# First chunk's pool mixer and layer norm ahead of the others, its first three FFN products between their stages

## The chip, the cores and the metric

The kernel runs on one core of a Trainium2 chip. The metric is the device time of one execution in microseconds (us). Engines are named as in the profile: PE (TensorE matmul), PEld (its weight loads), DVE (VectorE), ACT (ScalarE), POOL (GpSimd), and SP (SyncE), whose queue issues the DMA transfers.

## The reference

One inference step of a two-layer decoder trunk for 1024 prompt tokens, 16 meta tokens and 8 sample tokens, model width 1024, in float32. Layer 0 mixes by causal pooling (trailing means over 2, 4, 8 and 16 tokens in four groups of channels, each followed by a 256x256 projection); layer 1 by sliding-window attention. Every layer then has a gated FFN with a short convolution.

```python
mix = pool_mixer(x, w_pool, scale)          # window mean minus token, projected per group
x = layer_norm(ALPHA * x + mix, g, b)
gu = x @ w_in                               # 1024 -> 2 * 2816
g, u = gu[..., :D_FF], gu[..., D_FF:]
c = conv_b + sum(shift(g, k) * conv_w[k] for k in range(3))
h = silu(c) * u
x = layer_norm(ALPHA * x + h @ w_out, g2, b2)
...
```

## The kernel before, in words

Features lie on the 128 partitions, tokens on the free axis. The tokens are cut into three chunks: chunk 0 has 280 columns (16 meta, 8 samples, 256 prompt tokens), chunks 1 and 2 have 384 each. Every product of the FFN is three matmuls, because weights and activations are split into a high and a low part (`mm3`, lines 115 to 122). The high part of a weight is an ACT cast (line 111) and its low part a POOL subtraction (line 112), both from a raw tile that SP has loaded (line 105). Raw tiles have two buffers in all (tag `raw`), and the pool mixer's inputs (`praw`, line 247) use the same two.

The first phase makes, for each chunk in the order of the source:

- the pool mixer `pool_chunk` (line 273): running sums `pt` on DVE and POOL (line 292; group 3 and every third stage of a group are POOL's), the differences `pd` on DVE (lines 303 to 314), projections `pp` on PE (line 325), and `zp` on DVE (line 326). A chunk has eight `zp` tiles;
- the layer norm `ln_steps` (line 187): the mean `ps_mum` on PE (line 143), the subtraction (line 188, DVE), squares (line 192, ACT), the variance `ps_varm` on PE, the reciprocal root by Ln and Exp (lines 200 and 201, ACT), the scaling (line 224 on DVE, or line 211 on POOL for the tiles in `on_pool`), then the high part `xh` (line 232, ACT) and the low part `xl` (line 233 on DVE, line 222 on POOL).

Then `ffn(0)` (line 354) begins with the first three of 22 column blocks f of the FFN, chunk by chunk: `ffn1(f, c)` (line 361) makes the gate product `pg` and the up product `pu` with 24 matmuls each, copies the gate to SBUF (ACT), convolves it (POOL line 378, DVE lines 379 to 381 for chunk 0), and makes h (silu on ACT line 398, DVE lines 399 and 402, ACT line 401). From block 3 on the loops run block by block over all chunks, with the output products `po` between.

A scheduler orders the instructions of each engine at build time, from the order of the source and its own timing model; on the chip every engine runs its list in that order and waits where an input is missing. `tc.issue_after(ins)` keeps a block's instructions on the engine of `ins` behind it. In what follows a name such as `pt_1_0` carries the chunk and the tile, `pg_0_1` the block and the chunk; the last number of a name in an ordered list is that of a buffer.

Of the kernel before, what the change touches and what calls it, by code (L numbers as in the profile page):

```python
# [10 lines left out]
ALU = mybir.AluOpType  # L11
# [16 lines left out]
# prompt blocks (of 128 tokens) per chunk; the first chunk also carries the  # L28
# meta tokens and the sample tokens: columns [meta 16 | samples 8 | prompt]
# [6 lines left out]
# columns alive after the attention: [meta14 meta15 | samples 8 | prompt]  # L36
# [3 lines left out]
# packed per-partition constant columns  # L40
# [7 lines left out]
# constants of the first phase alone  # L48
# [11 lines left out]
def trunk_kernel(ctx: ExitStack, tc: tile.TileContext, ins: dict, outs: dict):  # L60
# [19 lines left out]
    # ------------------------------------------------------------ constants  # L80
# [34 lines left out]
    def mm3(out, wts, movs):  # L115
        """out += sum_k w_k^T x_k over exact hi/lo parts (all but lo*lo)."""
        n = len(wts)
        for k in range(n):
            (wh, wl), (mh, ml) = wts[k], movs[k]
            nc.tensor.matmul(out, lhsT=wh, rhs=mh, start=(k == 0), stop=False)  # L120
            nc.tensor.matmul(out, lhsT=wh, rhs=ml, start=False, stop=False)  # L121
            nc.tensor.matmul(out, lhsT=wl, rhs=mh, start=False, stop=(k == n - 1))  # L122
# [7 lines left out]
    # ----------------------------------------------------------- layer norm  # L130
    def colsum(parts, W, name, on_pe, own=False, split=False, pairs=False, step=KT):
        """mean over all features of 8 [P, W] tiles -> PSUM, on every partition; pauses after every step tiles."""
        ps = bank(f"ps_{name}", "ln")[:, :W]
        if on_pe:
            # fp32 products; with pairs, of sums of two tiles
            n = KT // 2 if pairs else KT
            for k in range(n):
                if pairs:
                    t = hslot([P, W], f"pr{k}_{name}", F32)
                    (nc.gpsimd if k < n // 2 else nc.vector).tensor_tensor(t, parts(2 * k), parts(2 * k + 1), ALU.add)  # L140
                else:
                    t = parts(k)
                nc.tensor.matmul(ps, lhsT=r32(ones), rhs=t, start=(k == 0), stop=(k == n - 1))
            return ps
        s = [None, None]
        for m in range(0, KT, 2):
            # two chains of sums, so that one is ready while the other's last ends
            i = m // 2 % 2
            a, b = parts(m), parts(m + 1)
            eng = nc.vector if split and i else nc.gpsimd  # L150
            if s[i] is None:
                s[i] = a if own else ltmp([P, W], f"s{i}_{name}")
                eng.tensor_tensor(s[i], a, b, ALU.add)
            else:
                eng.tensor_tensor(s[i], s[i], a, ALU.add)
                eng.tensor_tensor(s[i], s[i], b, ALU.add)
            if (m + 2) % step == 0 and m + 2 < KT:
                yield
# [19 lines left out]
    def ln_steps(z, W, lni, c, xo, name, out=None, on_pe=False, on_pool=(), lnexp=False, split=False, fin=False):  # L178
        # a list of tiles in the place of x, which gets new ones
# [18 lines left out]
        if lnexp:  # L198
            # both functions share a table set with the softmax's
            nc.scalar.activation(rstd, var, AF.Ln, bias=epsc)  # L200
            nc.scalar.activation(rstd, rstd, AF.Exp, scale=-0.5)
        else:
            nc.scalar.activation(rstd, var, AF.Sqrt, bias=epsc)
            nc.vector.reciprocal(rstd, rstd)
        yield
        for m in range(KT):
# [16 lines left out]
            else:  # L223
# [6 lines left out]
                else:  # L230
                    h, l = xh[c][m][:, xo:xo + W], xl[c][:, m, xo:xo + W]
                    nc.scalar.activation(h, zm, AF.Identity, bias=b)
                    nc.vector.scalar_tensor_tensor(l, zm, b, r32(h), ALU.add, ALU.subtract)
# [8 lines left out]
    # ------------------------------------------------------------ first loads  # L242
# [29 lines left out]
    # ------------------------------------------------------------ pool mixer  # L272
    def pool_chunk(c):
# [8 lines left out]
        def sums(g):  # L282
            raws[g] = raw0[:, 2 * g:2 * g + 2, :] if c == 0 else pool_raw(c, g)
            for kk in range(2):
# [4 lines left out]
                while sh < WINDOWS[g]:  # L289
                    lo += sh  # L290
                    eng = nc.gpsimd if g == 3 or sh == 4 else nc.vector
                    eng.tensor_tensor(bufs[i][:, lo:], cur[:, lo:], cur[:, lo - sh:HALO + Ws - sh], ALU.add)
                    cur, sh, i = bufs[i], sh * 2, 1 - i
                curs[k] = cur

        def rest(g):
# [9 lines left out]
            if c == 0:  # L306
                # samples: last w-1 state rows and the token itself
# [8 lines left out]
            # alpha * x  # L316
# [12 lines left out]
        for g in range(4):  # L329
            # in this order on the vector engine, whose first groups' loads land first  # L330
# [5 lines left out]
            next(r, 0)  # L336
        return z
# [4 lines left out]
    # ------------------------------------------------------------------- FFN  # L342
# [11 lines left out]
    def ffn(L, first_w):  # L354
# [67 lines left out]
        def ffn2_last(gi, c):  # L422
            """the last group: the sums of its first half run while the second half's h is made."""
# [31 lines left out]
        win = {0: first_w, 1: load_in(1), 2: load_in(2, "wo")}  # L455
        for c in range(NCH):
            for f in range(3):
                ffn1(f, c, *win[f])
        win[3] = load_in(3)
# [15 lines left out]
        for c in range(NCH):  # L475
# [7 lines left out]
            if c == NCH - 1:  # L483
                exp_tables()
                # the reciprocal root of the chunk before shares this chunk's table set
# [21 lines left out]
    # ---------------------------------------------------------- phase 1: pool  # L507
    first = None
    exp_tables()
    for c in range(NCH):  # L510
        z = pool_chunk(c)
        layer_norm(z, WX[c], 0, c, 0, f"m0{c}", on_pe=(c < 2), on_pool=(6, 7), lnexp=True)
        if c == 1:
            first = (load_w(ins["win"][0, 0], "g0_0"), load_w(ins["win"][0, NF], "u0_0"))
            ffn_pre(0)
# [4 lines left out]
    ffn(0, first)  # L520

    # ------------------------------------------------- pass-through state rows
# [7 lines left out]
    # ------------------------------------------------------------ shared K / V  # L530
# [57 lines left out]
    # --------------------------------------------------------------- attention  # L588
    O = {}

    class Q:
        """query projection of head pair t for one chunk, issued in slices."""
# [19 lines left out]
        def finish(self):  # L612
# [5 lines left out]
            # one engine after the other: they take turns at a bank  # L618
# [11 lines left out]
    def att_s(u, q):  # L630
# [10 lines left out]
        # e = -s with the negated sink as its last column, mx = -max  # L641
# [43 lines left out]
    def load_state(i):  # L685
        """state keys and values of kv heads 2i and 2i+1; slot 0 holds the new token."""
# [7 lines left out]
    def att_virtual(i, kv):  # L694
        """the 8 samples and the last two meta tokens, for kv heads 2i and 2i+1."""
# [52 lines left out]
    def o_piece(c, half, m, w, z):  # L748
        """half of the output projection's sum, for output tile m."""
# [6 lines left out]
        if half == 0:  # L756
# [3 lines left out]
            # the sum takes the place of x  # L760
# [5 lines left out]
    def later_kv():  # L766
        """the later chunks' keys and values, made beside the first units."""
# [16 lines left out]
    # slots of 512 columns for the transposed weights; the first query weights pass through  # L784
# [15 lines left out]
    # output projection: (first unit, chunk, half, tile); the weights of a pair of tiles come ahead  # L800
# [76 lines left out]
def _lay_out(inputs):  # L877
# [5 lines left out]
    def fm(x):  # L883
        """[tokens, features] -> [partition, feature tile, token]"""
# [20 lines left out]
    # heads in pairs: pair 4c+g holds head g of kv head 2c, then of kv head 2c+1  # L905
# [3 lines left out]
    # [half of the pairs, pair of output tiles, partition, (output tile, head pair, column)]  # L909
# [19 lines left out]
    # constants of the shapes alone  # L929
# [46 lines left out]
```

## Time and profile before

| | |
|---|---|
| three runs | 2005.25, 2007.79, 2009.0 us |
| median | 2007.79 us |
| span of the profiled execution, first to last instruction | 2004.4 us |
| PE busy | 1932.9 us, 96% |
| DVE busy | 1263.3 us, 63% |
| POOL busy | 813.9 us, 41% |
| granted PE clock, mean over the span | 0.986 |

The page gives of the profiled execution its span, with no other time beside it; the median of the runs is 3.4 us above that span. The span falls into a first phase, in which PE has gaps, and a rest, in which it has almost none.

### The profile page before, as it was taken

What the parts mean: (1) busy time and instruction counts of PE and PEld (TensorE: products, weight loads), DVE (VectorE), ACT (ScalarE), POOL (GpSimd) and SP (SyncE); (2) the same over time, 40 slices, a digit from 0 to 9 for tenths busy, and PEclk for the clock granted to TensorE, in tenths of its full rate; (3) what the DMA queues carried; (4) which work ended last, traced back from release to release, by engine and by line L of the source; (5) the groups of instructions that cost most, each with busy time, mean ns of one, the idle gap of its engine ahead of it and who ended that gap; (6) DMA issues with size and microseconds to landing.
All of it is one profiled execution on the core that took longest, in us unless ns stands there. A gap on an engine that the chain in (4) does not pass through costs nothing. (4 is left out here: it accounts for less than half of the span.)

```text
span 2004.4 us, 31349 instructions
## 1 busy us (share of the span) xinstructions
PE 1932.9 (96%) x12208; PEld 1896.3 (95%) x12208; DVE 1263.3 (63%) x2367; ACT 712.3 (36%) x1585; POOL 813.9 (41%) x880
## 2 busy tenths in 40 slices
PE   6899999999999999899999989999999999999997
PEld 4699999999999999889999988999999999999996
DVE  7977545454544456887989896675445454544566
ACT  2452122112211221476778784512122112212234
POOL 6752334214321432653464657533143224322333
PEclk9899999999999999999999999999999999999998
DMA  5201111101110111314343322011011011101102
GB/s 194 78 22 43 53 54 63 43 22 64 64 37 27 64 53 34 30 49 148 107 132 102 109 81 85 32 51 55 33 64 55 31 42 63 54 32 43 64 23 65
DMA packets 50422, 123.45 MB, mean 62 GB/s; under 512 B 11481, under 2 KB 25489, under 8 KB 50217
## 3 DMA queue, kind: packets, MB, share of 16 engines
q1 hardware_dynamic: 50272, 121.44, 19.6%
q8 instruction: 96, 1.57, 0.3%
q14 instruction: 54, 0.43, 0.1%
HBM read 108.29 MB, written 7.54 MB: 58 GB/s over the span
## 5 line engine op out<-in xcount | busy, mean ns | idle before, releaser
L112 POOL TENSOR_TENSOR w_wo<-raw_wo,w_wo 128x512 fp32r<-128x512 f32 (+1 forms) x92 | 169.3, 1859 | 550.9 <-ACT w_wo L111 548.0
L121 PE MATMUL pg<-xl,w_g 128*128 128x384 f32 (+2 forms) x1056 | 337.4, 319 | 0.0
L121 PE MATMUL pu<-xl,w_u 128*128 128x384 f32 (+2 forms) x1056 | 336.6, 319 | 0.0
L420 DVE TENSOR_TENSOR acc<-acc,po 128x384 f32<-128x384 f32 (+2 forms) x432 | 222.1, 515 | 173.8 <-PE po L122 170.9
L121 PE MATMUL po<-h,w_wo 128*128 128x384 f32 (+2 forms) x960 | 305.9, 319 | 0.0
L120 PE MATMUL po<-h,w_wo 128*128 128x384 f32 (+2 forms) x960 | 305.7, 318 | 0.0
L122 PE MATMUL po<-h,w_wo 128*128 128x384 f32 (+2 forms) x960 | 305.6, 318 | 0.0
L111 ACT CAST w_wo<-raw_wo 128x512 fp32r<-128x512 f32 (+1 forms) x92 | 71.6, 822 | 422.4 <-PE po L122 417.6
L402 DVE TENSOR_TENSOR h<-c,h 128x280 fp32r<-128x280 f32 (+2 forms) x132 | 147.7, 1119 | 88.3 <-ACT h L401 87.7
L392 POOL TENSOR_SCALAR c<-g,cols 128x384 f32<-128x384 f32 (+1 forms) x110 | 80.2, 729 | 294.6 <-issue 281.6
L121 PEld LDWEIGHTS pg<-xl,w_g 128*128 128x128 f32 x1056 | 198.8, 188 | 0.1
L121 PEld LDWEIGHTS pu<-xl,w_u 128*128 128x128 f32 x1056 | 198.3, 188 | 0.0
L393 DVE SCALAR_TENSOR_TENSOR c<-g,cols,c 128x384 f32<-128x384 f32 (+1 forms) x110 | 67.8, 616 | 194.4 <-POOL c L392 194.4
L122 PEld LDWEIGHTS po<-h,w_wo 128*128 128x128 f32 x960 | 180.4, 188 | 0.0
L120 PEld LDWEIGHTS po<-h,w_wo 128*128 128x128 f32 x960 | 180.3, 188 | 0.0
L121 PEld LDWEIGHTS po<-h,w_wo 128*128 128x128 f32 x960 | 180.1, 188 | 0.0
L398 ACT ACTIVATE c<-c 128x280 f32<-128x280 f32 (+2 forms) x132 | 65.1, 493 | 312.4 <-DVE c L394 277.5
L120 PE MATMUL pg<-xh,w_g 128*128 128x384 f32 (+1 forms) x528 | 170.1, 322 | 0.0
L122 PE MATMUL pg<-xh,w_g 128*128 128x384 f32 (+1 forms) x528 | 169.1, 320 | 0.0
L120 PE MATMUL pu<-xh,w_u 128*128 128x384 f32 (+1 forms) x528 | 168.9, 320 | 0.0
L122 PE MATMUL pu<-xh,w_u 128*128 128x384 f32 (+1 forms) x528 | 168.8, 320 | 0.0
L120 PE MATMUL pg<-xa,w_g 128*128 128x384 f32 (+1 forms) x528 | 168.6, 319 | 0.0
(270 smaller groups left out, 4673.5 us busy)
## 6 DMA issues: line engine op xcount, KB each, us to landing
raw_g<-in_win SPq DMA_DIRECT2D x44, 512.0 KB, 3.5
raw_u<-in_win SPq DMA_DIRECT2D x44, 512.0 KB, 3.5
raw_wo<-in_wout SPq DMA_DIRECT2D x44, 512.0 KB, 3.5
raw_wq<-in_wq SPq DMA_DIRECT2D x24, 512.0 KB, 3.5
raw_wo<-in_wo SPq DMA_DIRECT2D x24, 512.0 KB, 3.6
q<-q SPq DMA_DIRECT2D x64, 96.0 KB, 2.1
praw<-in_xq SPq DMA_DIRECT2D x8, 400.0 KB, 5.4
out_yT<-acc SPq DMA_DIRECT2D x8, 384.0 KB, 2.5
```

The source lines that it names most:

```text
L111: nc.scalar.copy(w[:, 0, s], raw[:, s])
L112: nc.gpsimd.tensor_tensor(w[:, 1, s], raw[:, s], r32(w[:, 0, s]), ALU.subtract)
L120: nc.tensor.matmul(out, lhsT=wh, rhs=mh, start=(k == 0), stop=False)
L121: nc.tensor.matmul(out, lhsT=wh, rhs=ml, start=False, stop=False)
L122: nc.tensor.matmul(out, lhsT=wl, rhs=mh, start=False, stop=(k == n - 1))
L392: nc.gpsimd.tensor_scalar(cc, g[:, 0:n], w0, b, ALU.mult, ALU.add)
L393: nc.vector.scalar_tensor_tensor(cc, g[:, 1:1 + n], w1, cc, ALU.mult, ALU.add)
L398: nc.scalar.activation(ct, ct, AF.Silu)
L402: nc.vector.tensor_tensor(ht[:, 1, :], ct, r32(ht[:, 0, :]), ALU.subtract)
L420: nc.vector.tensor_tensor(a, a, ps, ALU.add)
```

## The change

The chunk loop of the first phase is taken apart. Chunk 0's pool mixer is traced first, then the loads of the first FFN weights, then chunk 0's layer norm, with all eight tiles scaled and split on DVE and ACT (before, tiles 6 and 7 were POOL's). `ffn(0)` follows at once and takes two functions: after `ffn1(0, 0)` it calls `second`, which traces pool mixer and layer norm of chunk 1, and after `ffn1(1, 0)` it calls `third`, which does so for chunk 2. The weights of blocks 1 and 2 are loaded where they are first needed. The pool mixer of chunk 1 is kept behind chunk 0's last `pd` on DVE and last running sum on POOL, that of chunk 2 behind chunk 0's last `xl` on DVE and chunk 1's last running sum on POOL.

```diff
-    def ffn(L, first_w):
+    def ffn(L, first_w, between=()):
...
-        win = {0: first_w, 1: load_in(1), 2: load_in(2, "wo")}
+        between = iter(between)
+        win = {0: first_w}
         for c in range(NCH):
             for f in range(3):
+                if f not in win:
+                    win[f] = load_in(f, "wo" if f == 2 else "w")
                 ffn1(f, c, *win[f])
+                next(between, lambda: None)()
...
-    for c in range(NCH):
-        z = pool_chunk(c)
-        layer_norm(z, WX[c], 0, c, 0, f"m0{c}", on_pe=(c < 2), on_pool=(6, 7), lnexp=True)
-        if c == 1:
-            first = (load_w(ins["win"][0, 0], "g0_0"), load_w(ins["win"][0, NF], "u0_0"))
-            ffn_pre(0)
+    def chunk_norm(c, z):
+        layer_norm(z, WX[c], 0, c, 0, f"m0{c}", on_pe=(c < 2), on_pool=(6, 7) if c else (), lnexp=True)
+    z0 = pool_chunk(0)
+    pd, sums = mark["DVE"], mark["POOL"]
+    first = (load_w(ins["win"][0, 0], "g0_0"), load_w(ins["win"][0, NF], "u0_0"))
+    chunk_norm(0, z0)
+    fin = mark["DVE"]
+    ffn_pre(0)
+    def second():
+        with behind(pd, sums):
+            z = pool_chunk(1)
+        chunk_norm(1, z)
+    def third():
+        with behind(fin, mark["POOL"]):
+            z = pool_chunk(2)
+        chunk_norm(2, z)
...
-    ffn(0, first)
+    ffn(0, first, (second, third))
```

On DVE, in the middle of chunk 0's pool mixer, the list before has chunk 1's running sums (`pt_1_...`) among chunk 0's differences:

```order
L314 SCALAR_TENSOR_TENSOR pd_2_197<-dsm,cols_105 128x2x8
L292 TENSOR_TENSOR pt_1_0_327<-praw_0_325 128x399
L292 TENSOR_TENSOR pt_1_1_329<-praw_0_325 128x399
L304 TENSOR_TENSOR pd_2_197<-pd_2_197,raw_100 128x16
L292 TENSOR_TENSOR pt_1_2_345<-praw_1_343 128x399
L326 SCALAR_TENSOR_TENSOR zp_120<-pp_2_179,cols,zp_120 128x280
```

In the change the same sums stand behind chunk 0's whole layer norm and behind the convolution of its first FFN product (`t_0_0`, `c_0_0`):

```order
L391 SCALAR_TENSOR_TENSOR t_0_0_385<-g_0_0_380,cols,t_0_0_385 128x272
L392 SCALAR_TENSOR_TENSOR c_0_0_379<-g_0_0_380,cols,t_0_0_385 128x16
L393 SCALAR_TENSOR_TENSOR c_0_0_379<-g_0_0_380,cols,t_0_0_385 128x256
L301 TENSOR_TENSOR pt_1_0_414<-praw_0_412 128x399
L301 TENSOR_TENSOR pt_1_1_416<-praw_0_412 128x399
L301 TENSOR_TENSOR pt_1_2_432<-praw_1_430 128x399
```

So chunk 1's sums no longer run among chunk 0's steps, and DVE reaches them only when `g_0_0`, a copy of a finished product, is there. POOL's list has the same turn: `t_0_0`, then `pt_1_6`.

On SP, the change's loads after the first inputs and the pass-through copies stand so; `praw_..` with three digits behind it are chunk 1's (398 to 452) and chunk 2's (638 to 692) inputs:

```order
L256 DMA praw_2_452<-in_xq 128x2x400
L114 DMA raw_g_1_559<-in_win 128x1024
L114 DMA raw_u_1_564<-in_win 128x1024
L256 DMA praw_0_652<-in_xq 128x2x400
L256 DMA praw_1_670<-in_xq 128x2x400
L256 DMA praw_2_692<-in_xq 128x2x400
L114 DMA raw_g_2_811<-in_win 128x1024
L114 DMA raw_u_2_816<-in_win 128x1024
```

Before, all `praw` loads of chunks 1 and 2 stood ahead of the weights of blocks 1 and 2; now the last of chunk 2's stands between the weights of block 1 and those of block 2. All take turns at the two raw buffers.

On PE, chunk 0's third block (`pg_2_0`) now stands behind the first halves of chunk 2's last projections (`pp_4` to `pp_7`, from chunk 2's `pd`); behind it come `pu_2_0` and only then chunk 1's first product, `pg_0_1`:

```order
L336 MATMUL pp_2_684<-pd_1_680,pw_102 128x384
L336 MATMUL pp_3_688<-pd_1_680,pw_102 128x384
L336 MATMUL pp_4_708<-pd_2_704,pw_103 128x384
L336 MATMUL pp_5_712<-pd_2_704,pw_103 128x384
L336 MATMUL pp_6_720<-pd_3_716,pw_104 128x384
L336 MATMUL pp_7_724<-pd_3_716,pw_104 128x384
L129 MATMUL pg_2_0_821<-xh_0_73,w_g_2_813 128x280
```

Before, all projections of all chunks stood ahead of the first FFN product, `pg_0_0`; now `pg_0_0` and `pu_0_0` stand ahead of chunk 1's first projection, and the third block waits for chunk 2's.

## Rows read from the trace of the kernel before

**Rows 1.** Page, engines over the span: busy us (share) and instructions.
```profile
PE 1932.9 (96%) x12208; PEld 1896.3 (95%) x12208; DVE 1263.3 (63%) x2367; ACT 712.3 (36%) x1585; POOL 813.9 (41%) x880
```
**Rows 2.** Waits of PE from 150 us on: us in total, times, longest.
```profile
PE po L433 <- DVE acc L441: 5.2, 2, 2.8
```
**Rows 3.** Stretches: length, busy us (count) by engine, granted PE clock, DMA share, GB/s.
```profile
70.00:80.00 10.00, 6.70 (x17) 4.27 (x18) 10.00 (x13) 4.11 (x9) 5.71 (x3) 0.53 0.40 135
110.00:152.00 42.00, 42.00 (x245) 42.00 (x244) 28.86 (x37) 21.19 (x37) 21.72 (x28) 1.00 0.08 26
```
**Rows 4.** Timeline of PE: start, duration, engine and line, operation, [idle before <- releaser].
```profile
73.30 5.49 PE L325 MATMUL pp<-pd,pw 128*128 128x384 f32 x8 [6.30 <-DVE zp L326]
...
78.02 1.01 PE L120 MATMUL pg<-xh,w_g 128*128 128x280 f32 x1
...
102.38 0.33 PE L120 MATMUL pg<-xh,w_g 128*128 128x384 f32 x1
...
127.72 0.33 PE L120 MATMUL pg<-xh,w_g 128*128 128x384 f32 x1
...
152.68 0.29 PE L120 MATMUL pg<-xh,w_g 128*128 128x280 f32 x1
```
**Rows 5.** Timelines of DVE and POOL, a DVE step alone and one beside a weight split.
```profile
117.85 0.62 DVE L394 SCALAR_TENSOR_TENSOR c<-g,cols,c 128x384 f32<-128x384 f32 x1
134.59 2.71 POOL L112 TENSOR_TENSOR w_g<-raw_g,w_g 128x1024 fp32r<-128x1024 f32 x1
135.08 2.64 DVE L394 SCALAR_TENSOR_TENSOR c<-g,cols,c 128x384 f32<-128x384 f32 x1
```
**Rows 6.** Timeline of POOL: chunk 1's eight running sums, first and last five.
```profile
19.66 1.26 POOL L292 TENSOR_TENSOR pt<-praw 128x399 f32<-128x399 f32 x1
...
23.25 5.47 POOL L292 TENSOR_TENSOR pt<-pt 128x393 f32<-128x393 f32 x5
```
**Rows 7.** Timeline of DVE from chunk 0's pool mixer to its layer norm.
```profile
18.32 0.44 DVE L292 TENSOR_TENSOR pt<-pt 128x285 f32<-128x285 f32 x1
32.14 0.16 DVE L314 SCALAR_TENSOR_TENSOR pd<-dsm,cols 128x16 f32<-128x16 f32 x1
36.53 0.51 DVE L326 SCALAR_TENSOR_TENSOR zp<-pp,cols,zp 128x280 f32<-128x280 f32 x1
42.65 2.92 DVE L188 TENSOR_TENSOR zp<-zp,ps_mum 128x280 f32<-128x280 f32 x8
```
**Rows 8.** Loads: issue on SP, and the ACT step that waited for the landing.
```profile
30.51 0.40 SPq L247 DMA_DIRECT2D praw<-in_xq  x1
33.75 0.84 ACT L317 ACTIVATE zp<-praw 128x768 f32<-128x768 f32 x1 [1.86 <-DMA praw<-in_xq]
57.12 0.34 SPq L105 DMA_DIRECT2D raw_g<-in_win  x1
60.64 1.05 ACT L111 CAST w_g<-raw_g 128x1024 fp32r<-128x1024 f32 x1 [3.40 <-DMA raw_g<-in_win]
```
**Rows 9.** Timeline of ACT: chunk 2's reciprocal root, with its table loads.
```profile
116.35 1.28 ACT L200 ACT_TABLE_LOAD   x1
117.64 0.58 ACT L200 ACTIVATE rstd_m<-ps_varm,epsc 128x384 f32<-128x384 f32 x1
118.24 1.28 ACT L201 ACT_TABLE_LOAD   x1
119.54 0.53 ACT L201 ACTIVATE rstd_m<-rstd_m 128x384 f32<-128x384 f32 x1
```
**Rows 10.** Timeline of DVE: layer norms of chunks 1 and 2.
```profile
61.59 3.79 DVE L188 TENSOR_TENSOR zp<-zp,ps_mum 128x384 f32<-128x384 f32 x8
84.19 6.56 DVE L224 SCALAR_TENSOR_TENSOR zp<-zp,cols,rstd_m 128x384 f32<-128x384 f32 x6 [2.64 <-ACT rstd_m L201]
92.11 5.00 DVE L233 SCALAR_TENSOR_TENSOR xl<-zp,cols,xh 128x384 fp32r<-128x384 f32 x5
124.81 0.61 DVE L233 SCALAR_TENSOR_TENSOR xl<-zp,cols,xh 128x384 fp32r<-128x384 f32 x1
```

More of the change, by code (lines that the diff above doesn't have):

```diff
@@ L78, in hslot, with behind @@
         return pool.tile(shape, dt, tag="h", bufs=12, name=name)
+    mark = {}
+    def behind(*ins):
+        st = ExitStack()
+        for i in ins:
+            st.enter_context(tc.issue_after(i))
+        return st
     cols = pool.tile([P, NCOL], F32, name="cols")
@@ L142, in colsum @@
                     t = parts(k)
-                nc.tensor.matmul(ps, lhsT=r32(ones), rhs=t, start=(k == 0), stop=(k == n - 1))
+                mark["PE"] = nc.tensor.matmul(ps, lhsT=r32(ones), rhs=t, start=(k == 0), stop=(k == n - 1)).ins
             return ps
@@ L232, in ln_steps @@
                     nc.scalar.activation(h, zm, AF.Identity, bias=b)
-                    nc.vector.scalar_tensor_tensor(l, zm, b, r32(h), ALU.add, ALU.subtract)
+                    mark["DVE"] = nc.vector.scalar_tensor_tensor(l, zm, b, r32(h), ALU.add, ALU.subtract).ins
             if m % 2 == 1:
@@ L291, in sums @@
                     eng = nc.gpsimd if g == 3 or sh == 4 else nc.vector
-                    eng.tensor_tensor(bufs[i][:, lo:], cur[:, lo:], cur[:, lo - sh:HALO + Ws - sh], ALU.add)
+                    a = eng.tensor_tensor(bufs[i][:, lo:], cur[:, lo:], cur[:, lo - sh:HALO + Ws - sh], ALU.add)
+                    if eng is nc.gpsimd:
+                        mark["POOL"] = a.ins
                     cur, sh, i = bufs[i], sh * 2, 1 - i
@@ L336, in pool_chunk @@
             next(r, 0)
+        mark["DVE"] = last[3]
         return z
@@ L505, in ffn @@
         nc.sync.dma_start(outs["ncs"][L], gs)
-    first = None
     exp_tables()
-    for c in range(NCH):
-        z = pool_chunk(c)
-        layer_norm(z, WX[c], 0, c, 0, f"m0{c}", on_pe=(c < 2), on_pool=(6, 7), lnexp=True)
-        if c == 1:
-            first = (load_w(ins["win"][0, 0], "g0_0"), load_w(ins["win"][0, NF], "u0_0"))
-            ffn_pre(0)
+    def chunk_norm(c, z):
[14 more added lines that the diff above has]
+        chunk_norm(2, z)
     for t, n in ((ident, "ident"), (mask, "mask"), (nsink, "sinkb")):
```

## The prediction, made before the changed kernel ran

> **What bounds the kernel now.** I read the page's shares first, then PE's waits, then the stretches and the timelines of the first 160 us. PE is busy for 96% of the span [rows 1], and from 150 us on its longest entry in the list of waits sums to 5.2 us in 1850 us [rows 2]. From 110 to 152 us it has no gap, at full clock [rows 3]. So the kernel is bound by PE from the moment it is fed without a break, and what a change of the first phase is worth is read from one mark: the start of block 3's first product, `pg_3_0`, at 152.68 us [rows 4]. From there on the lists of all engines hold the same work in the same order, and a shift of the mark goes through to the end.
>
> Ahead of it stand chunk 0's first FFN product (78.02), chunk 1's (102.38) and chunk 2's (127.72) [rows 4]. The last two intervals, 25.3 and 25.0 us, are three blocks of 48 products each, at 0.17 us a product, and hardly anything else. So the mark moves with chunk 1's first product, **M1**, which stands at 102.38.
>
> What sets M1 is DVE and POOL. The reader should see in [rows 5] that a DVE step of 0.62 us took 2.64 us beside a weight split on POOL: it ended when the split ended. Where both read SBUF they take turns, so in the first phase their times add up. Before, DVE had chunk 1's and 2's sums to do whenever chunk 0's layer norm made it wait. That filling is what the change takes away.
>
> **The change, step by step.** All times from the span's start. "Low" and "high" are the bounds.
>
> 1. Chunk 0's sums. The loads of the first weights now stand ahead of all chunk 1 loads on SP, so both splits come on POOL in front of two sums that DVE needs: two times 2.71 us [rows 5], less 0.4 that POOL was idle, 5 us (low 0, high 5.4). In exchange the stretch from 18.76 (end of the first row of [rows 7]) to the last `zp` tile at 37.04 loses 14 DVE steps of chunk 1, 6.6 us at the 0.47 of eight steps in 3.79 us [rows 10], and the turns of POOL's eight sums, which ran from 19.66 to 28.72 [rows 6]; I take 3 us for those (0 to 6). Of the rest, 4.4 us from the last difference at 32.14 to the last tile's start at 36.53 are projections on a slow PE [rows 7]. The last tile: 18.8 + 5 + 18.3 - 6.6 - 3 = 32.5 (28 to 36).
> 2. Chunk 0's norm, with nothing between its steps: subtractions 2.9 us [rows 7], eight scalings at the same pace 2.9, Ln and Exp 1.1 (the activations of [rows 9] without the loads), and by estimate 3.6 for the mean's and the variance's last products and the first low part. Chunk 0's first product comes at **43** instead of 78.02 (39 to 47). The two tiles moved from POOL to DVE are among the eight.
> 3. 37 products until `pg_0_0` is whole: 4.8 us at 0.13, 9.6 at half clock. After a gap of 6.30 us PE's eight projections took 5.49 us and the granted clock of that stretch was 0.53 [rows 3, 4], which is near the lower level, so I take 6.5. Then the copies, POOL's step and three convolution steps, 2.2 us. All that time DVE has nothing it may do: its next entries are those steps, and chunk 1's sums stand behind them. POOL's do too. They start at 51.7 (low 7 us after step 2, high 11.8) instead of 19.66 [rows 6].
> 4. POOL's eight sums and DVE's steps take turns for 9 us, as in [rows 6] (6 to 12): 60.7.
> 5. Only now chunk 1's first `praw` tile is free, and `praw_2` is issued into it. A load takes 3.2 us from issue to the step that waited for it [rows 8]: 64.0. DVE is idle.
> 6. Sixteen DVE steps to the last `zp` of chunk 1, 7.6 us at 0.47, plus a hold of 2.7 by the split of `w_g_1` and one of 1.1 by a POOL sum [rows 5, 6]: 75.4 (8 to 13 us).
> 7. The last products of the mean stand behind 24 of chunk 0's second block on PE (3.1 us, or 6.2 on a slow PE); DVE's subtraction stands behind a sum whose `praw` tile is loaded only after the split of `w_u_1`. I take 8.6 us, 84 (4 to 10.5).
> 8. Subtraction 3.8 [rows 10], three steps to the cast of `h_1_0` 1.6, then the reciprocal root. Silu has pushed the table out, so two loads come in: 1.28 + 0.58 + 1.28 + 0.53 [rows 9], with the cast 4.2: 93.6 (91 to 95). On ACT the two loads are added work on the path. The Trainium skill's page ScalarE: Activation LUTs, section What ACT_TABLE_LOAD costs, gives 2.66 us for a switch, with a drain; two would put the sum 2.8 us higher. In [rows 9] the next activation starts 1.29 us after the load does, so the sum goes by 1.28.
> 9. Scalings 6.6 in turns with POOL [rows 10], then four differences of chunk 2, 2.6 (together 5 to 11): 102.8.
> 10. Those free the raw tile for `raw_g_2`. Load 3.5, cast 1.05, split 2.71; that frees the one for `raw_u_2`, again 3.5, 1.05 and 2.71 [rows 5, 8]: 14.5, at 117.3 (113 to 121). Chunk 1's low parts, 5 us for five [rows 10], are done at about 108; but on PE `pg_2_0` waits for chunk 2's differences, behind those low parts, and `pu_2_0` for this split.
> 11. 24 products of `pu_2_0`: 3.1 us. **M1 at about 120** instead of 102.4.
> 12. Chunk 2's variance products stand 30 products later behind M1 than before, 5.2 us at 0.17. Before, its first low part was ready at 125.42 [rows 10] for a product at 127.72 [rows 4], 2.3 us to spare. So PE waits some 2.5 us more (0 to 4).
>
> The mark: 120 + 25.3 + 25.0 + 2.5 = 172.8, which is 20 us later than 152.68. The profiled execution's span is 2004.4; the runs' median is 2007.79, so 3.4 above it, and I add the 20 to the median: **2028 us**. All bounds low together give M1 at 92, all high at 144; as they are independent, the root of the sum of the squared half widths, some 9 us, is the likeliest case's own range: 2019 to 2037.
>
> Not counted, because it is hidden: the pass-through copies stand where they stood, ahead of what waits; from block 3 on weights are loaded long ahead of use.
>
> **The rivals.** (a) *Faster.* PE has done all three blocks of chunk 0 (18.5 us) before chunk 1 is ready. Before, chunk 1's low parts ended at 97.1 [rows 10], and PE was still at chunk 0 until 102.4. If `w_u_2` is split before 99.3 and chunk 1 is ready by 92, M1 falls to about 92 and the end by 8 to 10 us, to 1997 to 2000. For it: chunk 0 is ready 35 us earlier. Against: chunk 1's sums start 32 us later on both engines, and three loads hang one behind the other on two tiles. It needs nearly every term at its low bound. (b) *No change or a small loss.* The turns cost half of what I take (steps 1, 4, 6, 9) and PE is fast in steps 3 and 7: M1 between 101 and 110, 2009 to 2018. For it: DVE steps that read PSUM, like the subtractions, keep 0.47 us each beside POOL. (c) *A greater loss.* PE works in pieces from 43 to 120 and its clock stays at the lower level: 3 us more in step 3, 3 in step 11 and some in the first of chunk 1's products, M1 at 126 to 130, 2034 to 2038. For it: 0.53 in [rows 3] after one gap. That the change does nothing is excluded by the lists of instructions.
>
> **How the numbers follow.** My case 0.67, (a) 0.08, (b) 0.13, (c) 0.12. A measurement here tells about 0.2% (4 us) from no change. Faster is (a) with 0.08; the same is nearly half of (b), 0.06; slower the rest, 0.86. The range from 2011 to 2036 leaves out (a), the lower part of (b) and the upper part of (c).
>
> **What would show it.** `pg_0_0` starts near 43; DVE is idle for some 5 us before chunk 1's first sum near 52, and again for a load near 61; two table loads in chunk 1's reciprocal root; PE waits with `pu_2_0` for a POOL split near 117; M1 near 120, `pg_3_0` near 173; behind it the same as before. I am wrong if M1 lies under 103, or if `pg_3_0` comes 20 us later and the end doesn't.

## The result, and the profile after

| | before | changed |
|---|---|---|
| median of the runs | 2008.39 us (4 runs) | 2040.94 us (4 runs) |
| span of the profiled execution | 2004.4 us | 2036.1 us |
| granted PE clock, mean | 0.986 | 0.983 |
| chunk 0's first FFN product | 78.02 us | 41.61 us |
| chunk 1's first FFN product, M1 | 102.38 us | 132.95 us |
| chunk 2's first low part, on DVE | 124.81 us | 161.02 us |
| block 3's first product, the mark | 152.68 us | 186.06 us |

The changed kernel is slower, by a ratio of 1.0162 with a 95% interval of 1.0148 to 1.0177. That is 32.5 us; the prediction had the sign, with a size of 20 us and a range to 2036.

The page's shares of the changed kernel, against [rows 1]:

```profile
PE 1937.2 (95%) x12208; PEld 1896.1 (93%) x12208; DVE 1265.8 (62%) x2371; ACT 716.6 (35%) x1586; POOL 808.2 (40%) x876
```

PE, DVE, ACT and POOL are each within 6 us of what they were busy before, in a span that is 31.7 us longer. The change added waiting, hardly any work. The timeline of PE (start, duration, engine and line, operation, the idle time before it and what ended that) shows where, against [rows 4]:

```profile
41.61 0.40 PE L129 MATMUL pg<-xh,w_g 128*128 128x280 f32 x1 [2.16 <-ACT xh L241]
...
62.37 8.49 PE L336 MATMUL pp<-pd,pw 128*128 128x384 f32 x16 [10.24 <-DVE pd L316]
...
106.08 7.13 PE L336 MATMUL pp<-pd,pw 128*128 128x384 f32 x16 [10.09 <-DVE pd L316]
119.86 4.47 PE L336 MATMUL pp<-pd,pw 128*128 128x384 f32 x8 [6.65 <-DVE pd L316]
...
132.95 0.33 PE L129 MATMUL pg<-xh,w_g 128*128 128x384 f32 x1
...
159.37 0.34 PE L129 MATMUL pg<-xh,w_g 128*128 128x384 f32 x1
161.68 0.45 PE L130 MATMUL pg<-xl,w_g 128*128 128x384 f32 x1 [1.97 <-DVE xl L242]
...
186.06 0.29 PE L129 MATMUL pg<-xh,w_g 128*128 128x280 f32 x1
```

Chunk 0's first product comes 36.4 us earlier, and that buys nothing: PE then waits for DVE's differences (`pd`) of chunks 1 and 2, and M1 is 30.6 us late. The 161.68 row is the second thing to see. When PE has done chunk 1's three blocks it has to wait once more, for chunk 2's first low part (`xl`). So at the mark two chains meet, one over M1 and one over chunk 2's norm, and they are 31 and 36 us late. Behind M1 PE has 288 products, 50.3 us; what the mark stands further behind M1 is nearly all waiting, here 2.8 us in total.

Behind the mark the two kernels run alike. The mark shifted by 33.4 us, the span by 31.7.

**Where the time went.** All of chunk 2's norm passes through DVE. So I counted what DVE did between 20 us and its first low part of chunk 2. The view of stretches gives the length, then the busy time of PE, PEld, DVE, ACT and POOL with counts, the clock, the DMA share and the rate. The kernel before, and then the changed one:

```profile
20.00:124.80 104.80, 90.79 (x420) 71.41 (x419) 93.66 (x151) 49.89 (x95) 71.88 (x70) 0.92 0.22 76
```

```profile
20.00:161.00 141.00, 101.35 (x444) 77.95 (x443) 97.45 (x163) 52.32 (x96) 65.36 (x69) 0.87 0.16 53
```

DVE was busy for 93.7 us before and for 97.5 now. It was idle for 104.8 - 93.7 = 11.1 us before and for 141.0 - 97.5 = 43.5 us now. Of the 36.2 us by which chunk 2's low part is late, 32.4 are idle time on DVE and 3.8 are added work or turns with POOL. The list of DVE's waits in the same stretches (total, times, longest) says what it was idle for. Before, the two longest entries were:

```profile
DVE zp L224 <- ACT rstd_m L201: 4.3, 2, 2.6
DVE pt L292 <- DMA praw<-in_xq: 2.2, 2, 1.2
```

and in the changed kernel the five longest:

```profile
DVE zp L233 <- ACT rstd_m L210: 12.8, 3, 6.0
DVE zp L337 <- PE pp L336: 8.8, 6, 4.1
DVE c L409 <- ACT gs L387: 8.5, 3, 3.8
DVE t L391 <- POOL t L390: 3.1, 3, 1.6
DVE pt L301 <- DMA praw<-in_xq: 2.4, 1, 2.4
```

DVE waits for the reciprocal root of each chunk, for projections, and for the copies (`gs`) of a gate product on PE. The same results were needed before, but at most of these places DVE then had sums and differences of another chunk in its list to do meanwhile. Now those stand behind the step that waits. For the reciprocal root it waited 4.3 us in two pieces before and none of it for chunk 0; now it is 12.8 us in three, 6.0 of them for chunk 0.

### The profile page after: what moved, and what is told of

Read it like the earlier page. It is cut to its first block, busy times and chain, and to the rows that moved or that the text cites. A ratio compares the mean times of both kernels' runs of the same rounds, so it can differ in the third digit from the quotient of the medians.

```text
span 2036.1 us, 31361 instructions
## 1 busy us (share of the span) xinstructions
PE 1937.2 (95%) x12208; PEld 1896.1 (93%) x12208; DVE 1265.8 (62%) x2371; ACT 716.6 (35%) x1586; POOL 808.2 (40%) x876
## 4 chain that ended last, share of the span: by engine, by line
PE 78%; DVE 11%; ACT 4%; issue 3%; DMA 2%; POOL 1%; SPq 0%; DVEq 0%; ACTq 0%; POOLq 0%
PE pg L130 8%; PE pg L131 8%; PE pg L129 8%; PE pu L130 8%; PE pu L131 8%; PE pu L129 8%; PE po L130 7%; PE po L129 7%; PE po L131 7%; PE pq L638 2%; PE po L445 1%; DVE e L681 1%; DVE acc L233 1%; DMA praw<-in_xq 1%; DVE xl L242 1%
## 5 line engine op out<-in xcount | busy, mean ns | idle before, releaser
L129 PE MATMUL pu<-xh,w_u 128*128 128x384 f32 (+1 forms) x528 | 169.4, 321 | 0.0
```

## The experiments

Fourteen kernels ran. Each was timed beside the kernel before, whose median was 2005 to 2008 us in these comparisons; the ratios are to that, and a ratio is turned into us with 2008. Four words recur: M1, the mark, "first low part" (chunk 2's first on DVE) and "DVE idle" (its idle time from 20 us to that low part, from the view of stretches as above).

| run | ratio (95% interval) | M1 | first low part | DVE busy + idle | mark |
|---|---|---|---|---|---|
| before | 1 | 102.4 | 124.8 | 93.7 + 11.1 | 152.7 |
| changed | 1.0162 (1.0148 to 1.0177) | 133.0 | 161.0 | 97.5 + 43.5 | 186.1 |
| 1 stages ahead | 1.0069 (1.0049 to 1.0089) | 103.6 | 138.4 | 98.6 + 19.8 | 164.5 |
| 2 second ahead | 1.0064 (1.0047 to 1.0081) | 112.3 | 142.1 | 95.5 + 26.6 | 168.1 |
| 3 free slot | 1.0165 (1.0144 to 1.0186) | 131.4 | 159.5 | 99.4 + 40.1 | 184.5 |
| 4 third after block 2 | 1.0213 (1.0185 to 1.0241) | 133.9 | 168.4 | 96.2 + 52.2 | 195.8 |
| 5 third split | 1.0152 (1.0136 to 1.0167) | 120.9 | 157.1 | 95.6 + 41.5 | 184.3 |
| 6 early weights only | 1.0070 (1.0054 to 1.0087) | 103.7 | 139.7 | 97.6 + 22.1 | 166.2 |
| 7 stages ahead, POOL tiles | 1.0046 (1.0031 to 1.0060) | 110.1 | 136.1 | 99.1 + 17.0 | 162.7 |
| 8 chunk 2 after norm 0 | 1.0071 (1.0054 to 1.0089) | 119.1 | 140.3 | 89.7 + 30.6 | 169.4 |
| 9 filled PE | 1.0147 (1.0124 to 1.0169) | 129.5 | 157.4 | 98.0 + 39.4 | 182.5 |
| 10 weights, own tiles | 1.0081 (1.0061 to 1.0101) | 110.4 | 139.8 | 97.7 + 22.1 | 166.5 |
| 11 stages ahead, own tiles | 1.0089 (1.0068 to 1.0109) | 117.4 | 140.4 | 93.6 + 26.8 | 168.3 |
| 12 pool 1 ahead | 1.0106 (1.0087 to 1.0125) | 118.9 | 147.0 | 97.6 + 29.4 | 173.4 |
| 13 idle splits | 1.0049 (1.0028 to 1.0071) | 108.6 | 134.8 | 95.3 + 19.5 | 161.5 |
| 14 early weights, pinned | 1.0073 (1.0051 to 1.0094) | 103.8 | 138.3 | 97.8 + 20.5 | 164.7 |

Read the table down two columns. Busy and idle time of DVE add up to the first low part by the way they are counted; what the table shows is which of them varies. Busy is between 90 and 99 us in every kernel, idle between 11 and 52. And the mark stands 25 to 29 us behind chunk 2's first low part in every kernel. 25.0 of these are chunk 2's 144 products, so chunk 2's norm is never more than 4 us from being what PE waits for; in the kernel before it was 2.3 us ahead [rows 4, 10]. But it isn't what PE waits for everywhere: in the kernel before and in runs 8 and 11 PE has no wait between M1 and the mark, which stand 50.3, 50.3 and 50.8 us apart, so there M1 sets the mark. In the other thirteen kernels PE waits in between for chunk 2's norm.

**Run 1: both stages ahead of the FFN again.**

```diff
-    ffn(0, first, (second, third))
+    second()
+    third()
+    ffn(0, first)
```

> The changed kernel, with the second and third chunks' pools and norms called ahead of the FFN again (the early weight loads, the first chunk's norm on DVE alone and the late loads of the other weights all stay). Theory A (the loss is the filling that the first and second chunk's norm waits lost): DVE and POOL take chunk 1's sums in those waits again; M1 (start of chunk 1's first FFN product) at 97 to 104, the mark at 148 to 155, time 2003 to 2012. Theory B (the loss comes from the two weight splits ahead of chunk 0's sums and the reordered norm): M1 stays above 120, time above 2028.

Between the two theories. M1 is back at 103.6, as theory A had it, yet the time is 1.0069, some 14 us above before and not level with it. The place of the stages in the source makes about 19 us of the 32.5 (1.0162 - 1.0069). The early weights and what came with them make the rest, and they do it through chunk 2, not through M1.

**Run 2: only the second stage ahead.**

```diff
-    ffn(0, first, (second, third))
+    second()
+    ffn(0, first, (third,))
```

> The changed kernel with only the second chunk's stage called ahead of the FFN; the third one stays behind the first product. Theory A: chunk 0's norm waits are filled by chunk 1's sums, chunk 1's by nothing: DVE loses only the waits from 82 us on, M1 at 108 to 120, time 2012 to 2025. Theory B: as the changed kernel, above 2035.

Theory A, in its range at 2020.07 us. It stands level with run 1 (mark and first low part are 3.6 and 3.7 us later, the ratio is not higher), so that a third stage behind the first product costs little or nothing once the second one is ahead. In the changed kernel the third stage stands behind the second product. Run 12 divides the second stage further.

**Run 3: the slot of block 2's up weights.** `praw` of group 3 moved from the buffers of the weights into the space of `xl2`, which is free until chunk 2's norm.

```diff
...
-        raw = pool.tile([P, 2, Wr], F32, tag="wo" if g == 3 else "raw", bufs=2, name=f"praw{c}_{g}")
+        raw = praw3[:, c - 1] if g == 3 else pool.tile([P, 2, Wr], F32, tag="raw", bufs=2, name=f"praw{c}_{g}")
...
```

> The changed kernel, with the group 3 tiles of chunks 1 and 2 in the space of chunk 2's low parts, so that block 2's up weights no longer take a tile that chunk 2's last difference frees. Theory A2 (PE's queue sets M1: block 2's gate product stands behind chunk 2's last four projections): the split of w_u_2 ends some 2 us earlier, M1 stays at 132 to 134, time within 2 us of the changed kernel, 2038 to 2043. Theory C (the chain of loads and splits of block 2's weights sets M1, as step 10 of the prediction had it): M1 falls by 2.5 to 5 us, time 2035 to 2038.

In the changed kernel, on ACT and on POOL:

```profile
122.12 1.04 ACT L120 CAST w_u<-raw_u 128x1024 fp32r<-128x1024 f32 x1 [8.21 <-DVE pd L316]
```

```profile
123.25 2.37 POOL L121 TENSOR_TENSOR w_u<-raw_u,w_u 128x1024 fp32r<-128x1024 f32 x1 [1.57 <-ACT w_u L120]
```

The cast of `w_u_2` had waited 8.21 us for a tile that chunk 2's last differences held. In run 3 the same split starts earlier:

```profile
118.93 2.66 POOL L122 TENSOR_TENSOR w_u<-raw_u,w_u 128x1024 fp32r<-128x1024 f32 x1
```

That is 4.3 us earlier, and M1 moved by 1.5, of which 1.3 were there from chunk 0's first product on (40.30 instead of 41.61). Theory A2: the chain of loads and splits that step 10 of the prediction priced isn't what M1 waits for.

**Run 4: the third stage one product later.** On top of run 3:

```diff
-    ffn(0, first, (second, third))
+    ffn(0, first, (second, lambda: None, third))
```

> As the run before it, and the third chunk's stage called after the first chunk's third FFN product instead of after the second: block 2's products of chunk 0 stand ahead of chunk 2's pool on PE. Theory A2: M1 follows chunk 1's last low part and falls to 105 to 118; the mark then hangs on chunk 2's norm and falls less, to 172 to 182; time 2026 to 2036. Theory A3 (DVE's and POOL's idle time in the source's order is what counts, and a later third stage only moves more of it): the mark stays at 184 or rises, time 2038 to 2050.

The rival A3, 1 us above its range: M1 didn't fall, since the projections of chunk 2 only moved from in front of block 2 to in front of M1 itself, DVE's idle time rose to 52.2 us, and the time to 2051.22. One more product of chunk 0 ahead of a stage cost DVE 12 us more of idle time than in run 3.

**Run 5: the third stage in two parts.** Sums and differences between the second and third product, projections and norm after the third; block 2's weights ahead of it; the tiles of run 3.

```diff
...
-    ffn(0, first, (second, third))
+    got = []
+    ffn(0, first, (second, lambda: got.append(third()), lambda: third_b(got[0])))
```

> The changed kernel with the group 3 tiles in the space of chunk 2's low parts, block 2's weights loaded ahead of chunk 2's pool, and the third stage cut in two: sums and differences stay between the second and third product, projections and norm come after the third. On PE block 2's products of chunk 0 now stand ahead of all of chunk 2's projections. Theory A2 (M1 is late because those products stand behind projections that wait for DVE): M1 falls from 131 to 133 to the time of chunk 1's first low parts, 108 to 116; the mark falls to 165 to 177, time 2018 to 2031. Theory A3 (chunk 2's norm, fed by DVE and POOL, sets the mark anyway): M1 falls, but PE waits for chunk 2's low parts what M1 gained; mark 182 to 188, time 2034 to 2042.

A3, with M1 at 120.9; A2 had 108 to 116. PE's row of chunk 1's first product, its later waits and the mark:

```profile
120.91 0.41 PE L130 MATMUL pg<-xh,w_g 128*128 128x384 f32 x1 [0.53 <-DVE zp L345]
...
153.71 0.69 PE L130 MATMUL pg<-xh,w_g 128*128 128x384 f32 x1 [5.54 <-ACT xh L242]
...
158.47 0.69 PE L131 MATMUL pg<-xl,w_g 128*128 128x384 f32 x1 [2.48 <-DVE xl L243]
...
184.31 0.29 PE L130 MATMUL pg<-xh,w_g 128*128 128x280 f32 x1
```

M1 came 12 us earlier and the mark 1.8. PE had to wait for chunk 2's high and low parts, and what M1 had won was gone. So M1 doesn't decide the mark here.

**Run 6: the early weights in the kernel before.**

```diff
-        layer_norm(z, WX[c], 0, c, 0, f"m0{c}", on_pe=(c < 2), on_pool=(6, 7), lnexp=True)
-        if c == 1:
+        if c == 0:
             first = (load_w(ins["win"][0, 0], "g0_0"), load_w(ins["win"][0, NF], "u0_0"))
+        layer_norm(z, WX[c], 0, c, 0, f"m0{c}", on_pe=(c < 2), on_pool=(6, 7), lnexp=True)
+        if c == 0:
             ffn_pre(0)
```

> The kernel before with one edit: the first two weights are loaded and split right behind the first chunk's pool (and the state rows' products behind its norm), as in the changed kernel. Theory B (what is left of the loss when the stages stand ahead of the FFN, 12 us in the second run of this study, is the price of the two early splits, which hold DVE in chunk 0's sums): first product 5 us later than before at 83, mark 160 to 166, time 2015 to 2022. Theory D (that rest comes from the first chunk's norm on DVE alone or from the ordering edges): no change, 2004 to 2011.

The time is theory B's but for 0.7 us, 2022.69. Its path isn't: chunk 0's first product didn't come 5 us later (77.2 against 78.0) and M1 is 1.4 us later, but chunk 2's first low part is 14.9 us later. 11.0 of that are DVE's idle time.

**Run 7: run 1 with tiles 6 and 7 of chunk 0's norm on POOL again.**

```diff
-on_pool=(6, 7) if c else (), lnexp=True)
+on_pool=(6, 7), lnexp=True)
```

> The first run of this study (stages called ahead of the FFN) with tiles 6 and 7 of the first chunk's norm on POOL again, so that only the early weights and the ordering edges are left of the change. Theory B: within 3 us of that run, 2017 to 2023. Theory D (two scalings and low parts more on DVE make the rest): 2006 to 2013.

Just below theory B's range, at 2016.85. The two tiles on DVE make at most some 5 us of run 1's 14 (1.0069 - 1.0046; the intervals overlap, and the mark moved by 1.8). The rest lies with the early weights, the later loads of blocks 1 and 2, and the ordering edges. In the changed kernel the edges make nothing: without them every engine's list of instructions stays the same. In runs 1 and 7 they do change the lists, so what they cost there isn't shown.

**Run 8: one ordering edge in the kernel before.**

```diff
...
-        z = pool_chunk(c)
+        with tc.issue_after(fin_of[0]) if c == 2 else nullcontext():
+            z = pool_chunk(c)
```

> The kernel before with one ordering edge: chunk 2's pool may be placed only behind the first chunk's last low part, nothing else moved. If filling counts by who is filled (chunk 2's sums now fill chunk 1's norm instead of chunk 0's), chunk 0's first product comes at 65 to 75 instead of 78, chunk 1's norm is held up by chunk 2's sums, M1 stays at 98 to 106 and the time within 5 us of before, 2003 to 2013. If an uncovered wait in chunk 0's norm costs what it lasts, 2013 to 2025.

The second alternative, at 2022.44. Chunk 2's sums no longer fill chunk 0's norm, DVE's idle time goes from 11.1 to 30.6 us, and nothing is won for chunk 0 (its first product is at 91.5). DVE's longest wait, and chunk 2's last differences, which ended at 61.67 in the kernel before:

```profile
57.13 2.87 DVE L189 TENSOR_TENSOR zp<-zp,ps_mum 128x384 f32<-128x384 f32 x6 [8.31 <-PE ps_mum L143]
...
86.45 5.24 DVE L306 SCALAR_TENSOR_TENSOR pd<-pt,praw 128x384 f32<-128x384 f32 x4
```

This is the lost filling alone, in a kernel that has none of the change's other edits. It reaches the mark by another way than in the changed kernel, though: chunk 0's first product stands on PE behind all but the last of chunk 2's projections, which wait for these differences, so M1 comes 16.7 us later and the mark as much.

**Run 9: PE kept busy.** 12, 16 and 50 products of 512 columns into a bank that nothing reads, in three of PE's waits of the first 62 us.

```diff
...
+    def fill(name, after, n):
+        ps = bank(f"fill{name}")
+        with tc.issue_after(after):
+            for i in range(n):
+                nc.tensor.matmul(ps, lhsT=ones, rhs=first[0][:, 0, :512], start=(i == 0), stop=(i == n - 1))
...
+    fill("a", mu, 12)
...
+    fill("b", mark["PE"], 16)
...
+        fill("c", mark["MM"], 50)
```

> The changed kernel with 78 idle products of 512 columns on TensorE, 12 behind the first chunk's mean, 16 behind its variance, 50 behind its first FFN product: they keep TensorE busy where it waited for VectorE at the lower clock, and compute nothing that is used. Theory C (the lower clock of a TensorE that is fed in pieces is a main part of the loss): time 2020 to 2030. Theory A3 (VectorE's idle time in the source's order): the first chunk's norm and first product come 3 to 6 us earlier, chunk 1's sums with them, and the rest of the idle time stays; mark at 180 to 184, time 2034 to 2040.

A3, by time (2035.84) and mark (182.5). Chunk 0 gained less than it said: its first product starts at 41.88 instead of 41.61, since the second filling ran until 42.04, and DVE's first sum of chunk 1 came 1.5 us earlier, at 53.47. The two stretches of the changed kernel and of this run (the clock is the first number behind the busy times):

```profile
50.00:60.00 10.00, 2.13 (x17) 1.90 (x15) 8.15 (x10) 2.66 (x6) 8.41 (x10) 0.75 0.00 0
60.00:70.00 10.00, 7.63 (x14) 4.29 (x15) 7.56 (x15) 1.89 (x2) 2.33 (x4) 0.57 0.28 93
```

```profile
50.00:60.00 10.00, 10.00 (x44) 8.08 (x43) 9.43 (x11) 2.15 (x3) 8.96 (x10) 1.00 0.00 1
60.00:70.00 10.00, 8.36 (x27) 4.50 (x25) 7.59 (x12) 1.89 (x2) 3.58 (x4) 1.00 0.28 93
```

The granted clock stood at full, 2.4 GHz, through both, where it had been 0.75 and, near the lower level, 0.57. The mark came 3.6 us earlier, the ratio is 1.0147 (intervals overlap). So the lower clock up to 70 us makes some 3 of the 32.5 us. From 100 to 120 us nothing was filled (0.64 and 0.51 in this run, 0.52 and 0.82 in the changed kernel), and what the clock costs there no run shows. For the projections that stand ahead of block 2 an estimate from rows of the changed kernel is under 2 us: eight products took 4.47 us at 119.86 and eight more 2.74 at 125.86.

**Runs 10 and 11: raw tiles of their own for the first weights**, in run 6 and in run 7, so that chunk 1's first loads needn't wait for theirs.

```diff
...
-first = (load_w(ins["win"][0, 0], "g0_0"), load_w(ins["win"][0, NF], "u0_0"))
+first = (load_w(ins["win"][0, 0], "g0_0", raw=raw01[:, 0]), load_w(ins["win"][0, NF], "u0_0", raw=raw01[:, 1]))
...
```

> The kernel before with the early weight loads of the sixth run, but their raw tiles in the space of chunk 2's low parts, so that they take no raw tile from chunk 1's loads. Theory E (the early weights cost 14 us because chunk 1's first two loads wait for the two tiles): chunk 1's sums start at 20 again, first low part of chunk 2 at 124 to 130, time 2004 to 2012. Theory B (the two splits on POOL, ahead of sums that VectorE waits for, and their turns): 2015 to 2022.

> The seventh run (stages ahead of the FFN, POOL's two tiles kept) with the first weights' raw tiles in the space of chunk 2's low parts. Theory E: 2004 to 2011, within 3 us of the kernel before. Theory B: 2014 to 2018 as without.

Theory E fell in both, with 2023.54 and 2025.22; theory B's ranges were passed too, by 1.5 and 7 us. In run 10 DVE's first sum of chunk 1 came 13.5 us earlier than in run 6 (23.48 against 36.94), and the first low part stayed where it was (139.8 against 139.7). So the wait for raw tiles isn't the cost of the early weights. Run 11 is even slower than run 7: loads that come earlier gave another order of the lists, with chunk 0's first product at 95.1 us and 26.8 us of DVE idle instead of 17.0.

**Run 12: chunk 1's pool ahead, its norm where the change put it.**

```diff
+    with behind(pd, sums):
+        z1 = pool_chunk(1)
+
     def second():
-        with behind(pd, sums):
-            z = pool_chunk(1)
-        chunk_norm(1, z)
+        chunk_norm(1, z1)
```

> The changed kernel with only the second chunk's pool called ahead of the FFN; its norm and the whole third stage stay where the change put them. Theory A3: chunk 1's sums fill the first chunk's norm again, some 15 us of VectorE's idle time go, chunk 2's first low part at 142 to 150, mark 168 to 176, time 2018 to 2026. Rival (a stage's place matters as a whole, sums and norm): above 2032.

Theory A3, 2 us above its range with 2028.09 (the ratio stands for 21 us): 14.1 us of DVE's idle time went, the first low part came 14.0 us earlier. Against run 2 there are 8 us left. They aren't chunk 1's norm alone: in run 2 the third stage stands a product earlier as well, and no run parts the two. One more product ahead of the third stage cost 12 us of DVE's idle time in run 4.

**Runs 13 and 14: why the early weights cost 9 to 14 us.** Run 13 adds two loads, casts and splits behind chunk 0's pool of the kernel before, that nothing uses:

```diff
...
+        if c == 0:
+            for f in (0, NF):
+                nc.sync.dma_start(idle[:, 0], ins["win"][0, f])
+                nc.scalar.copy(idle[:, 1], idle[:, 0])
+                nc.gpsimd.tensor_tensor(idle[:, 2], idle[:, 0], idle[:, 1], ALU.subtract)
...
```

> The kernel before, its weights where they were, with two more loads, casts and POOL splits of the same size behind the first chunk's pool, into space that is free until chunk 2's low parts; nothing reads what they make. Theory B (the early weights cost 14 us by what their two splits hold up at 14 to 22 us): VectorE's idle time rises by some 5 to 10 us, mark at 160 to 166, time 2015 to 2022. Theory F (they cost it because the first chunk's FFN steps come ahead of chunk 1's norm in VectorE's list and wait there): the added splits cost what VectorE loses beside them, 2 to 5 us, time 2006 to 2012.

Run 14 is run 6 with the convolution steps of the first block behind chunk 1's last low part:

```diff
...
-                nc.vector.scalar_tensor_tensor(t1, g[:, 1:1 + ns], w1, t1, ALU.mult, ALU.add)
+                with tc.issue_after(fin_of[1]) if f == 0 else nullcontext():
+                    nc.vector.scalar_tensor_tensor(t1, g[:, 1:1 + ns], w1, t1, ALU.mult, ALU.add)
...
```

> The sixth run (the kernel before with the early weights) with the convolution steps of the first FFN block on VectorE placed behind chunk 1's last low part. Theory F: the wait of 6.0 us for the copies of that block's gate product goes, chunk 1's low parts at 97 instead of 103.5, chunk 2's first low part at 130 to 135, time 2012 to 2017. Theory B: the wait is replaced by another, 2019 to 2024.

Theory B in both, 2017.27 and 2020.11. In run 6 DVE had this wait ahead of chunk 1's scalings, and in run 14 that one:

```profile
90.14 2.34 DVE L397 SCALAR_TENSOR_TENSOR c<-gs,cols,pre 128x8 f32<-128x8 f32 x1 [6.02 <-ACT gs L375]
```

```profile
91.53 5.73 DVE L225 SCALAR_TENSOR_TENSOR zp<-zp,cols,rstd_m 128x384 f32<-128x384 f32 x6 [7.33 <-ACT rstd_m L202]
97.18 7.82 DVE L234 SCALAR_TENSOR_TENSOR xl<-zp,cols,xh 128x384 fp32r<-128x384 f32 x6
```

With the wait for the copies gone DVE waits in the same place for chunk 1's reciprocal root. Chunk 1's low parts do start at 97.18 as theory F had it, but take 7.82 us, and chunk 2 gains 1.4. What stays open is how the 9 to 14 us of the early weights divide. Added splits alone cost 10, but the second of them landed at 34.3 us and not near 19, since the two share their space; so run 13 isn't the same load on POOL at the same time.

No run beat the kernel before. It has the least idle time on DVE of all sixteen.

## Why the prediction was right and wrong

The sign and the reason were right: chunk 1's and 2's sums had filled the waits of chunk 0's norm, and the change took that away. Runs 8, 12 and 1 show with one edit each that this place of the sums costs DVE idle time and the kernel time. They don't show all of the loss: some 14 of the 32.5 us stay when the stages are ahead again (run 1), and how those arise is open. By its steps:

- **Steps 1 to 5** held to some 2 us. The last `zp` tile ends at 30.68 (32.5 forecast), chunk 0's first product at 41.61 (43), POOL's sums at 52.09 (51.7) and end at 60.57 (60.7), the sum that waits for `praw_2` starts at 66.12 (64.0).
- **Steps 6 and 7** were 5 us too short. The last `zp` steps of chunk 1 start at 78.58, after waits for projections on PE, and the mean's subtraction at 89.41 instead of 84. Between them DVE had one more wait, which step 7 didn't price:

```profile
83.37 0.23 DVE L409 SCALAR_TENSOR_TENSOR c<-gs,cols,pre 128x8 f32<-128x8 f32 x1 [3.60 <-ACT gs L387]
84.39 1.20 DVE L391 SCALAR_TENSOR_TENSOR t<-g,cols,t 128x272 f32<-128x272 f32 x1 [0.79 <-POOL t L390]
...
89.41 3.80 DVE L197 TENSOR_TENSOR zp<-zp,ps_mum 128x384 f32<-128x384 f32 x8
```

  The product that is copied was whole at 81.70. The copies start at 83.12, because on ACT they stand behind a step of chunk 2's pool that starts at 82.37, after 3.06 us of waiting for its load. Chunk 0's second block delays chunk 1's norm just as its first delays chunk 1's sums. The Trainium skill, page PSUM — Partial Sum Buffer, section Engine vs sequencer instructions, says that the queues of ScalarE, VectorE and GpSimd are strictly first in, first out. The trace agrees, by these 1.4 us between the product and its copies.
- **Step 8** held: from the subtraction's start to the scalings 9.40 us, 9.6 forecast. The two table loads came in, at 95.06 and 96.95, and each next activation started 1.30 us after the load began. So the trace doesn't show the 2.66 us that the Trainium skill's page ScalarE: Activation LUTs, section What ACT_TABLE_LOAD costs, gives with a drain.
- **Step 9** took 10.2 us instead of 9.2: scalings from 98.81, four differences to 109.0.
- **Steps 10 and 11 failed**: of the 13 us between M1 and its forecast 6 stood already at the end of step 9, and 7 came here, from another wait. They let `pu_2_0` follow the split of `w_u_2`. In PE's list 35 of the 48 products of block 2 stand behind chunk 2's last four products of projection and all 48 behind the twelve ahead of those, and their differences DVE makes only from 118.58 to 122.56, after chunk 1's low parts, four `zp` steps and more sums. Step 9 had priced only the first four of the eight difference steps. Run 3 shortened the chain that step 10 priced by 4 us, and M1 moved by 1.5.
- **Step 12 is the one that the size hangs on.** It added 2.5 us for chunk 2 to a mark that was worked out from M1, and the wait did come as 2.8 (186.06 - 132.95 - 50.3). That agreement is luck: both chains came late, by 31 and 36 us. Chunk 2's norm is a chain of its own, which I didn't work out to its end: its first low part at 161.0 gives the mark 25 us later, and an M1 that comes earlier only makes PE wait longer. Run 5 shows it: there M1 came at 120.9, within 1 us of the forecast, and the mark still stood at 184.3, not at 172.8. (That run also moved chunk 2's projections and norm a product later, and its first low part still came at 157.1 instead of 161.0.) Of the 13 us by which M1 was late, the 6 up to the end of step 9 lie ahead of chunk 2's norm in DVE's list too, so they delayed both chains. The sum should have taken the later of two chains, and the second one with DVE's idle time in it, 43.5 us by then instead of 11.1.

**The rivals.** (a) Chunk 0's head start would win: chunk 0 was ready 36 us earlier, and run 2 shows why that is worth nothing, with chunk 0 at 52 and the mark at 168. (b) Small loss: excluded by the time. (c) PE's clock: its time, 2034 to 2038, lies nearest to the measured one, but its mechanism didn't carry the loss: filling PE's first waits gave back 3 us (run 9), and `pu_2_0`, which it had 3 us slower, ran at full clock, 24 products in 3.1 us.

**What the parts cost**, as differences of ratios, each uncertain by some 5 us: chunk 1's pool behind the first product 11 (changed less run 12); its norm there, together with a third stage one product later, 8 (run 12 less run 2); a third stage behind the first product about nothing (run 2 less run 1); two tiles from POOL to DVE 5, not clear of noise (run 1 less run 7); the early weights with the edges and the later loads of blocks 1 and 2, 9 (run 7).

## What to carry to other kernels

Where engines take their work in a fixed order, moving a chunk's start forward can cost the engine that serves all chunks whatever it now waits for with nothing else in its list to do: count that engine's busy and idle time up to the last chunk's need, before and after, and not the first chunk's readiness. Where several chains meet at one mark, work each out to its end; the one that looks covered by 2 us may be the bound, as in thirteen of these sixteen kernels. And a weight that is loaded earlier than needed isn't free: here it cost 14 us by itself (run 6), and two splits that nothing uses cost 10 (run 13), though by which wait stayed open.

## What was not expected

An ordering edge that moved no work into or out of the kernel cost 14 us (run 8), and a free tile for a load made the kernel slower (run 11 against run 7, 1.0089 and 1.0046): each gave the lists another order, and DVE's idle time was 19.5 us more in the one and 9.8 us more in the other. Filling PE's waits with 78 idle products raised its granted clock in 60 to 70 us from 0.57 to 1.00, and the variance products took 3.95 us instead of 5.93. But the products weren't quite free for what stood behind them: chunk 0's first product came 0.3 us later than without them.
